# Splitting the keys of a head pair in full-height operations, and filling the doubled tiles by half-token transfers

## The chip, the cores and the metric

The kernel runs on one core of one Trainium2 chip. The metric is the device time of one execution in microseconds (us). Before the change the median of three runs is 1488.08 us (1487.84 to 1490.82).

## What is computed

A two-layer encoder trunk over 1024 tokens of width 1024, in fp32. Layer 0 has global attention (8 query heads, 2 key heads), windowed attention (8 and 2) and attention into 256 memory tokens; layer 1 has 16 heads of neighbourhood attention on a 16 x 64 grid, and memory attention. The keys that the change concerns are those of the windowed attention (one pair of heads) and of the neighbourhood attention (eight pairs). The reference, cut to these:

```python
def reference(x, mem, ...):
    ...
        if l % 2 == 0:
            qa, ka, va, qb, kb, vb, qm, gate = split_cols(h @ w_in_even[e], SPLIT_EVEN)
            ...
            yb = window_gqa(qb.reshape(B, S, 8, 64), kb.reshape(B, S, 2, 64), vb.reshape(B, S, 2, 64), sink_b[e], rel_bias)
            ym = memory_attn(...)
            y = jnp.concatenate([ya, yb, ym], axis=-1) * jax.nn.silu(gate)
            x = x + y @ w_out_even[e]
        else:
            qc, kc, vc, qm, gate = split_cols(h @ w_in_odd[o], SPLIT_ODD)
            yc = neighborhood_attn(qc.reshape(B, S, 16, 64), kc.reshape(B, S, 16, 64), vc.reshape(B, S, 16, 64), rpb_c[o])
            ym = memory_attn(...)
            y = jnp.concatenate([yc, ym], axis=-1) * jax.nn.silu(gate)
            x = x + y @ w_out_odd[o]
    return rmsnorm(x, final_norm_gain)
```

## The kernel before, in words

Every fp32 operand of a matmul is kept as a high and a low part (fp32r); a product is the sum of high x high, high x low and low x high. TensorE (PE) does all products and transposes, ScalarE (ACT) copies the high part out of PSUM, VectorE (DVE) subtracts it from the source to get the low part, GpSimd (POOL) scales softmax rows and splits weights, SyncE (SP) issues nearly all transfers from one queue in program order.

A head has 64 channels, and a pair of heads fills 128 partitions. To do high and low of the query in one matmul, the query tile of a head holds its high part in one half of the partitions and its low part in the other; the key tile must then hold the same 64 key rows in both halves. So `k_pair` (line 345) makes four tiles of 128 x 1024 for a pair: high and low of head 0, high and low of head 1, each with its 64 rows twice. It projects 512 tokens at a time into a PSUM tile `pj`; for each 512 its `sink` makes, per head, a 64-row ACT copy (the high part, recorded at the helper's line L125) and a 64-row DVE subtraction (L361). After the second 512 four transfers of 64 x 1024 inside SBUF (L366 the high part, L367 the low, both named `k<-k`) copy each head's rows to the other half of its tiles.

`k_pair` is called once in layer 0 (`even`, with `natural=True`: the tokens are put in grid order, from an SBUF tile `vt`) and eight times in layer 1 (`keys(j)` in `odd`). There the projections of later pairs are broken in steps and run as filling work between the attention steps of the pair before. `near` runs the attention: scores of step n (`s<-k,q`, 16 steps a pair, 8 per head, head 0 first), softmax on DVE, ACT and POOL, transposes `tr<-ident,pn`, the split of the transposed rows into `ph` and `pl` (L125 and L542), products `pv`, and at the end of each half head `close`, whose DVE addition (L1158) writes the pair's output tile `yb`. There are two `yb` tiles, so a pair waits in `close` until the output of the pair two before it has left: `gated_steps` (line 470) gates it, sends the sums (L492), loads another pair's rows (L493), and sends two more differences (L500, and L503 which is the last to read `yb`).

The order of each engine's rows is fixed when the program is built, by a scheduler that goes by priorities and its own timeline; the queue of SP is in that order too, and a transfer that has to wait holds up all that stand behind it.

Of the kernel before, what the change touches and what calls it, by code (L numbers as in the profile page):

```python
# [9 lines left out]
F32 = mybir.dt.float32  # L10
# [3 lines left out]
OP = mybir.AluOpType  # L14
# [4 lines left out]
T = 1024  # L19
# [28 lines left out]
            c=(("P", "P"), ("P", "P"), ("P", "P"), ("yb", "yb"))),  # L48
       dict(y=(("P", "P", "q", "q", "v"), ("k", "k", "k", "k", "q", "q"), ("H",) * 6, ("H",) * 6, ("P", "P", "q", "q", "v"),
               ("k", "k", "k", "k", "q", "q"), ("H",) * 6),  # L50
            c=(("H", "H"), ("H", "H"), ("mk", "sg"), ("yb", "yb"))))
# [13 lines left out]
class Trunk:  # L65
# [279 lines left out]
    def k_pair(self, w, nt, natural=False):  # L345

        nc = self.nc
        ks = []

        def sink(p, c, n):  # L350
            if not ks:
                ks.extend([self.st("k", [128, T], F32R) for _ in range(2)] for _ in range(2))
            kh, kl = zip(*ks)
            p = self.with_rstd(p, c, n)[:, :n]
            if natural:
                p = p.rearrange("p (b r c) -> p b r c", r=16, c=8)
            for i in range(2):
                s = slice(64 * i, 64 * i + 64)
                h, l = (self.columns(t[i], c, n, natural) for t in (kh, kl))
                self.copy(h[s], p[s])  # L360
                nc.vector.tensor_tensor(l[s], p[s], h[s], op=OP.subtract)  # L361
            if c + n < T:
                return
            for i in range(2):
                s, o = slice(64 * i, 64 * i + 64), slice(64 - 64 * i, 128 - 64 * i)
                nc.sync.dma_start(kh[i][o, :].bitcast(F32), kh[i][s, :].bitcast(F32))  # L366
                nc.sync.dma_start(kl[i][o, :].bitcast(F32), kl[i][s, :].bitcast(F32))  # L367
        self.tokens(w, nt, sink)
        return ks

# [1851 lines left out]
```

## Time and profile before

| | |
|---|---|
| median of three runs | 1488.08 us |
| profiled execution: span from first to last instruction | 1486.8 us |
| around the span, against the median | 1.3 us |
| PE busy | 1467.6 us (99%) |
| DVE, ACT, POOL busy | 1030.7, 837.2, 644.2 us |
| transfers of the SP queue | 270.20 MB |
| neighbourhood attention and its key projections | about 1107 to 1357 us |

The profiled execution has no time of its own beside its span; 1.3 us is the median of the runs less the span, and is added to a span where a time is given. An instruction is named by engine, source line, output and inputs (`DVE L361 k<-pj,k` is the subtraction in `k_pair`). SPq is the queue of SP. In a list of waits or a timeline, `<-` and a name say what ended an engine's idle time. "To landing" is the time from the issue of a transfer to its arrival.

### The profile page before, as it was taken

The page shows a single profiled execution, that of the slowest core. Times are in us where ns is not written, and L with a number is a line of the kernel's source. Part 1 is how long each engine was busy: PE and PEld are TensorE (multiplying, and loading weights), DVE is VectorE, ACT ScalarE, POOL GpSimd, SP SyncE. Part 2 cuts the span into 40 slices and gives each one's busy share as a digit, 9 for nine tenths or more (in the row PEclk, how much of TensorE's full clock was granted, in tenths as well). Part 3 has the DMA queues.
Part 4 walks back from the last instruction along what each step waited for, and adds up shares of the span by engine and source line. Part 5 has one row for each costly group of instructions (what it writes and reads, how often), then busy time and mean ns, then how long its engine had stood idle before and what let it go on. Part 6 is the DMA issues. An engine that isn't in the chain of part 4 may idle for free.

```text
span 1486.8 us, 25511 instructions
## 1 busy us (share of the span) xinstructions
PE 1467.6 (99%) x8433; PEld 1274.7 (86%) x8433; DVE 1030.7 (69%) x2124; ACT 837.2 (56%) x1877; POOL 644.2 (43%) x767
## 2 busy tenths in 40 slices
PE   9999999999999999999999999999999999999998
PEld 8898898988888788888879987888998898888886
DVE  6687777677776577776687776664446787778674
ACT  7743665556655456654544444444446777777454
POOL 1223668556765746543450000001425556665454
PEclk9999999999999999999999999999999999999999
DMA  8966334434443424388553343567665568789834
GB/s 287 306 160 181 118 125 160 123 120 133 126 137 112 155 78 144 100 276 303 187 176 127 128 135 137 157 169 241 233 242 170 188 198 269 246 283 323 314 105 144
DMA packets 173860, 271.92 MB, mean 183 GB/s; under 512 B 15648, under 2 KB 96800, under 8 KB 172704
## 3 DMA queue, kind: packets, MB, share of 16 engines
q1 hardware_dynamic: 173296, 270.20, 56.4%
q8 instruction: 67, 1.10, 0.3%
q14 instruction: 65, 0.53, 0.1%
q10 hardware_dynamic: 432, 0.09, 0.0%
HBM read 174.28 MB, written 83.89 MB: 174 GB/s over the span
## 4 chain that ended last, share of the span: by engine, by line
PE 86%; DMA 6%; DVE 3%; ACT 2%; issue 1%; SPq 1%; POOL 1%; POOLq 0%; ACTq 0%; DVEq 0%
PE pj L242 16%; PE pj L62 11%; PE x L1617 6%; PE tr L133 6%; PE pv L1066 4%; PE y L1617 4%; PE pv L62 3%; PE s L62 3%; PE pj L1332 3%; PE tr L62 3%; PE sa L1332 2%; PE pv L1617 2%; PE sa L1033 2%; PE s L1332 2%; PE sa L1034 2%; PE pj L851 2%
## 5 line engine op out<-in xcount | busy, mean ns | idle before, releaser
L542 DVE TENSOR_TENSOR pl<-tr,ph 128x512 fp32r<-128x512 f32 (+2 forms) x352 | 203.9, 594 | 45.5 <-ACT ph L125 43.6
L125 ACT ACTIVATE ph<-tr 128x512 fp32r<-128x512 f32 (+2 forms) x352 | 176.2, 522 | 103.7 <-PE tr L133 79.7
L242 PE MATMUL pj<-H,wh 128*128 128x512 f32 x704 | 233.2, 411 | 0.6 <-DVE vt L313 0.2
L158 POOL TENSOR_SCALAR wh<-wraw 128x512 fp32r<-128x512 f32 x48 | 32.2, 673 | 275.2 <-PE x L1617 236.0
L125 ACT ACTIVATE wh<-wraw 128x384 fp32r<-128x384 f32 (+1 forms) x163 | 88.7, 553 | 99.6 <-PE pj L1332 12.2
L242 PE MATMUL pj<-H,wl 128*128 128x512 f32 x352 | 139.2, 395 | 0.0
L242 PEld LDWEIGHTS pj<-H,wh 128*128 128x128 f32 x704 | 120.6, 189 | 19.3 <-issue 0.6
L62 PE MATMUL pj<-H,wh 128*128 128x512 f32 x384 | 121.0, 396 | 0.0
L1119 POOL TENSOR_SCALAR pn<-pn,st 128x384 f32<-128x384 f32 (+1 forms) x128 | 72.7, 569 | 102.1 <-DVE st L1118 62.0
L133 PE MATMUL tr<-ident,P 128*128 128x128 f32 x752 | 115.4, 273 | 0.3 <-POOL P L719 0.2
L1279 POOL TENSOR_TENSOR wl<-wraw,wh 128x384 fp32r<-128x384 f32 x56 | 62.9, 1125 | 91.5 <-ACT wh L125 89.2
L1117 ACT ACTIVATE pn<-pn,st 128x384 f32<-128x384 f32 (+1 forms) x128 | 75.1, 587 | 41.8 <-DVE st L1114 40.5
L133 PEld LDWEIGHTS tr<-ident,P 128*128 128x128 f32 x752 | 88.9, 140 | 8.2 <-POOL P L719 1.2
L1039 ACT ACTIVATE P<-sa,st 128x1024 f32<-128x1024 f32 x64 | 71.4, 1117 | 35.3 <-PE tr L133 19.1
L1041 POOL TENSOR_SCALAR P<-P,st 128x1024 f32<-128x1024 f32 x64 | 74.6, 1169 | 27.9 <-DVE st L1040 27.3
L1038 DVE TENSOR_REDUCE st<-sa 128x1 f32<-128x1024 f32 x64 | 77.5, 1218 | 8.3 <-PE sa L1034 7.6
L62 PE MATMUL s<-k,q 128*128 128x384 f32 (+1 forms) x352 | 81.2, 327 | 0.0
L242 PEld LDWEIGHTS pj<-H,wl 128*128 128x128 f32 x352 | 66.2, 188 | 15.1
L62 PE MATMUL pj<-H,wl 128*128 128x512 f32 x192 | 75.6, 394 | 0.0
L160 POOL TENSOR_TENSOR wl<-wraw,wh 128x512 fp32r<-128x512 f32 x52 | 69.6, 1341 | 10.3 <-ACT wh L125 7.8
L851 PE MATMUL pj<-ah,H 128*128 128x256 f32 x384 | 70.8, 282 | 1.0 <-ACT ah L125 0.6
L62 PEld LDWEIGHTS pj<-H,wh 128*128 128x128 f32 x384 | 66.6, 188 | 5.4
(568 smaller groups left out, 4186.7 us busy)
## 6 DMA issues: line engine op xcount, KB each, us to landing
wraw<-w_o SPq DMA_DIRECT2D x52, 256.0 KB, 3.7
y<-yb SPq DMA_DIRECT2D x24, 512.0 KB, 3.4
wraw<-s SPq DMA_DIRECT2D x64, 192.0 KB, 3.9
wraw<-w_e SPq DMA_DIRECT2D x44, 256.0 KB, 3.3
k<-k SPq DMA_DIRECT2D x42, 256.0 KB, 5.9
s<-bias SPq DMA_DIRECT2D x56, 192.0 KB, 2.0
wq<-w_o SPq DMA_DIRECT2D x40, 256.0 KB, 3.3
y<-sg SPq DMA_DIRECT2D x18, 512.0 KB, 3.5
```

Source lines behind the costliest of these rows:

```text
L62: return lambda *a, **k: self.tc.keep_in_program_order(getattr(self.engine, name)(*a, **k))
L125: return self.nc.scalar.activation(out, in_, AF.Copy, scale=scale)
L133: self.turned = self.fence = self.pe.transpose(o, i, self.ident)
L242: self.pe.matmul(a[:, :n], s[:, kt % UNIT, :], m, start=(kt == 0 and i == 0), stop=(kt == KT - 1 and i == 2))
L542: self.low = nc.vector.tensor_tensor(pl[:, :n], tr[:, :n], ph[:, :n], op=OP.subtract)
L851: self.last = nc.tensor.matmul(a[:, b * 256:(b + 1) * 256], x[kt][:, t], w, start=(kt + b + i == 0), stop=(kt == KT - 1 and i == 2), skip_ ...
L1038: nc.vector.tensor_reduce(st[:, 0:1], s, axis=AX.X, op=OP.max, negate=True)
L1041: self.normal = nc.gpsimd.tensor_scalar(pt, pt, st[:, 2:3], 0.5, op0=OP.mult, op1=OP.mult)
L1117: nc.scalar.activation(o, o, AF.Exp, bias=st[:, 0:1], scale=-1.0, accum_out=st[:, 2:3])
L1119: self.normal = normal = nc.gpsimd.tensor_scalar(o, o, st[:, 3:4], 0.5, op0=OP.mult, op1=OP.mult)
L1332: last = nc.tensor.matmul(bank, s[:, k, :], y[3 * u + k][m][:, cols], start=start and u + k + e == 0, stop=u == 1 and k + e == 4, skip_gro ...
L1617: self.last = nc.tensor.matmul(bank, ws[s][:, k, :], b[k][m], start=start and k + i == 0, stop=k == UNIT - 1 and i == 2, skip_group_check= ...
```

## The change

`sink` now splits all 128 partitions at once: one ACT copy and one DVE subtraction for each 512 tokens (`split`, the helper at line 127), into the two tiles that will be head 1's. A new function `spread` then fills the other halves: `a` is a tile of head 0, `b` the tile of head 1 that holds both heads' rows. Head 0's rows go from `b` to the lower and to the upper half of `a`, and then head 1's rows go from the upper half of `b` to its lower half, over the rows just copied. This is done for the high part and then for the low part. In layer 1 `spread` is called after each 512 tokens (transfers of 64 x 512), in layer 0 once for all (64 x 1024). So a pair has 12 transfers of 128 KB in place of 4 of 256 KB in layer 1, and 6 of 256 KB in place of 4 in layer 0; the third of each three waits until the first two have landed, since it overwrites what they read.

```diff
         ks = []
+        one, two = slice(0, 64), slice(64, 128)
+
+        def spread(c):
+            for a, b in zip(*ks):
+                for t, o, f, i in ((a, one, b, one), (a, two, b, one), (b, one, b, two)):
+                    nc.sync.dma_start(t[o, c].bitcast(F32), f[i, c].bitcast(F32))
 
         def sink(p, c, n):
             if not ks:
                 ks.extend([self.st("k", [128, T], F32R) for _ in range(2)] for _ in range(2))
-            kh, kl = zip(*ks)
             p = self.with_rstd(p, c, n)[:, :n]
             if natural:
                 p = p.rearrange("p (b r c) -> p b r c", r=16, c=8)
-            for i in range(2):
-                s = slice(64 * i, 64 * i + 64)
-                h, l = (self.columns(t[i], c, n, natural) for t in (kh, kl))
-                self.copy(h[s], p[s])
-                nc.vector.tensor_tensor(l[s], p[s], h[s], op=OP.subtract)
-            if c + n < T:
-                return
-            for i in range(2):
-                s, o = slice(64 * i, 64 * i + 64), slice(64 - 64 * i, 128 - 64 * i)
-                nc.sync.dma_start(kh[i][o, :].bitcast(F32), kh[i][s, :].bitcast(F32))
-                nc.sync.dma_start(kl[i][o, :].bitcast(F32), kl[i][s, :].bitcast(F32))
+            self.split(*(self.columns(t, c, n, natural) for t in ks[1]), p)
+            if not natural:
+                spread(slice(c, c + n))
+            elif c + n == T:
+                spread(slice(0, T))
         self.tokens(w, nt, sink)
         return ks
```

The order of PE's rows is the same before and after. ACT and DVE each lose 18 rows, and a few rows beside them change places with a neighbour. The queue of SP gets 66 transfers more (33 listed rows, since two alike that follow each other stand in one row, marked x2) and is rearranged around them. Behind the changed function the line numbers are one lower after the change. Two places matter below.

The first is SP's queue at the start of `near`, where the first pair's keys are made. Before, `k_12667` and `k_12668` are the high and low tile of head 0, `k_12669` and `k_12670` those of head 1; `y_2` is an output row in DRAM, `qc` a stored query.

```order
L1019 DMA q_12894<-qc_9291 128x1024
L521 DMA y_2_85<-sg_12363 128x2x512
L520 DMA y_2_85<-yb_12362 128x2x512
L366 DMA k_12667<-k_12667 64x1024
L367 DMA k_12668<-k_12668 64x1024
L366 DMA k_12669<-k_12669 64x1024
L1989 DMA sg_12973<-g_9274 128x1024
L367 DMA k_12670<-k_12670 64x1024
L138 DMA wraw_13324<-w_o 128x512
```

The same place after; `k_12665` and `k_12666` are now the high and low tile of head 0 (`a`), `k_12667` and `k_12668` those of head 1 (`b`).

```order
L354 DMA k_12665<-k_12667 64x512 x2
L354 DMA k_12666<-k_12668 64x512 x2
L519 DMA y_2_85<-yb_12360 128x2x512
L520 DMA y_2_85<-sg_12361 128x2x512
L1018 DMA q_12900<-qc_9289 128x1024
L354 DMA k_12667<-k_12667 64x512
L354 DMA k_12665<-k_12667 64x512
L354 DMA k_12668<-k_12668 64x512
L354 DMA k_12665<-k_12667 64x512
L354 DMA k_12666<-k_12668 64x512 x2
L1988 DMA sg_12979<-g_9272 128x1024
```

The first half's transfers now stand ahead of the three 512 KB transfers, and two that wait for landings (`k_12667<-k_12667`, `k_12668<-k_12668`) stand ahead of or between those that complete head 0.

The second is SP's queue where the last pair's keys are made. `y_8` is the output whose store frees the `yb` tile for the seventh pair's `close`; the loads from `y_0` to `y_2` are the output projection's first operands. Before:

```order
L492 DMA y_8_91<-yb_14699 128x1024
L493 DMA sg_14737<-y_2_85 128x1024
L1231 DMA k_16037<-y_0_83 128x1024
L1019 DMA v_15687<-v_106 128x2048
L1231 DMA k_16038<-y_1_84 128x1024
L1081 DMA bm_15650<-offsets 128x640
L1231 DMA q_16039<-y_2_85 128x1024
L1291 DMA wraw_16269<-w_oo 128x384
L500 DMA y_8_91<-sg_14737 128x1024
L503 DMA y_8_91<-yb_14699 128x512
L366 DMA k_15597<-k_15597 64x1024
L367 DMA k_15598<-k_15598 64x1024
```

And after:

```order
L354 DMA k_15623<-k_15625 64x512 x2
L354 DMA k_15624<-k_15626 64x512 x2
L1080 DMA bm_15680<-offsets 128x640
L1018 DMA v_15717<-v_106 128x2048
L1230 DMA k_16067<-y_0_83 128x1024
L354 DMA k_15625<-k_15625 64x512
L354 DMA k_15626<-k_15626 64x512
L1230 DMA k_16068<-y_1_84 128x1024
L1230 DMA q_16069<-y_2_85 128x1024
L1290 DMA wraw_16299<-w_oo 128x384
L499 DMA y_8_91<-sg_14759 128x1024
L502 DMA y_8_91<-yb_14721 128x512
```

The two rows `y_8<-yb` and `sg<-y_2` that open the first list stand just ahead of this one too. Six transfers of the first half (0.75 MB) now stand ahead of the last store of `y_8`; the four that complete head 0 (`k_15623` and `k_15624`) follow right behind it, where two of 256 KB stood.

## The prediction

> **What bounds the kernel now.** I read the page first, then PE's waits in the stretch where eight of the nine key pairs are made (1100 to 1330 us), then the busy times there.
>
> ```profile
> PE 1467.6 (99%) x8433; PEld 1274.7 (86%) x8433; DVE 1030.7 (69%) x2124; ACT 837.2 (56%) x1877; POOL 644.2 (43%) x767
> ```
> ```profile
> PE tr L62 <- DVE pl L542: 0.9, 2, 0.6
> ```
> ```profile
> 1107.00:1125.00 18.00, 18.00 (x104) 15.64 (x103) 9.45 (x21) 10.12 (x27) 4.00 (x6) 1.00 0.87 298
> 1297.00:1327.40 30.40, 29.82 (x179) 26.34 (x178) 24.77 (x77) 22.74 (x62) 19.02 (x25) 1.00 0.74 250
> ```
>
> The first row says that PE is the bound. The wait list of the stretch holds this one line (who waits and for whom, us in total, times, longest): in 230 us PE waited 0.9 us, in two places. The window rows give stretch, length and busy time of PE, weight loads, DVE, ACT, POOL (instructions in brackets), then granted clock, DMA share and GB/s. PE is busy 18.00 of 18.00 us where the first pair is made and misses 0.58 us in the stretch that ends at the last pair, at a granted clock of 1.00. So PE's work, which the change leaves alone row for row, sets the time; only new PE waits or those 0.9 us can move it there.
>
> **The change, part by part.** First the operations that go. These are groups of DVE and ACT by shape, with count, busy us and mean ns.
>
> ```profile
> L361 DVE TENSOR_TENSOR k<-pj,k 64x512 fp32r<-64x512 f32 x32 | 22.0, 686 | 5.9 <-ACT k L125 5.4
> L313 DVE TENSOR_TENSOR vt<-pj,rows 128x512 f32<-128x512 f32 x10 | 6.8, 685 | 8.8 <-PE pj L242 8.8
> L125 ACT ACTIVATE k<-pj 64x512 fp32r<-64x512 f32 x32 | 18.9, 591 | 8.8 <-PE pj L62 7.1 <-DVE k L361 1.1
> L125 ACT ACTIVATE ph<-tr 128x512 fp32r<-128x512 f32 x184 | 109.1, 596 | 74.4 <-PE tr L133 71.8 <-issue 0.2
> L361 DVE TENSOR_TENSOR k<-vt,k 64x512 fp32r<-64x512 f32 x4 | 3.5, 867 | 1.4 <-ACT k L125 1.3
> L125 ACT ACTIVATE k<-vt 64x512 fp32r<-64x512 f32 x4 | 2.5, 629 | 0.1
> ```
>
> Full height costs no more than half height (685 against 686 ns on DVE, 596 against 591 on ACT). So half of each group goes: DVE 16 x 0.686 + 2 x 0.867 = 12.7 us, ACT 16 x 0.591 + 2 x 0.629 = 10.7 us. All of it lies beside a busy PE, so it gives PE at most its waits of 0.9 us; I count it as nothing. If that cover were gone it would be worth those 12.7 us, but no row shows PE waiting for a `k` split.
>
> In layer 0 the two added transfers and their waits come at about 490 us. Head 0's tile, which is read first, needs no waiting transfer, and what is queued behind them are weights loaded ahead of their split and stores. I cost it at zero; if a load there were late by a landing without cover, PE would lose up to the 6.4 us quoted below.
>
> Next the transfers of layer 1: 1.5 MB a pair for 1.0 MB. The queue that carries them is full at the first and the last pair and has gaps between (DMA share 1.00 and 0.99 there):
>
> ```profile
> 1107.00:1118.40 11.40, 11.40 (x68) 9.93 (x67) 7.04 (x14) 7.15 (x21) 3.69 (x5) 1.00 1.00 372
> 1307.80:1312.00 4.20, 4.20 (x29) 3.71 (x28) 4.00 (x11) 3.17 (x9) 1.17 (x2) 1.00 0.79 268
> 1312.00:1326.00 14.00, 14.00 (x83) 12.29 (x81) 10.98 (x36) 10.37 (x28) 9.18 (x12) 1.00 0.99 346
> ```
>
> First pair. SP's timeline (start, us) and PE's first scores of `near`, then the same transfers' size and time to landing:
>
> ```profile
> 1109.15 0.37 SPq L521 DMA_DIRECT2D y<-sg  x1
> 1109.87 0.37 SPq L520 DMA_DIRECT2D y<-yb  x1
> 1115.11 0.51 SPq L366 DMA_DIRECT2D k<-k  x1
> 1115.83 0.50 SPq L367 DMA_DIRECT2D k<-k  x1
> 1122.88 0.40 PE L62 MATMUL s<-k,q 128*128 128x256 f32 x2
> ```
> ```profile
> y<-sg SPq DMA_DIRECT2D x1, 512.0 KB, 7.9
> y<-yb SPq DMA_DIRECT2D x1, 512.0 KB, 8.5
> ```
> ```profile
> k<-k SPq DMA_DIRECT2D x1, 256.0 KB, 4.3
> ```
> ```profile
> k<-k SPq DMA_DIRECT2D x1, 256.0 KB, 4.7
> ```
>
> Issue plus landing: the stores arrive at 1117.05 and 1118.4, head 0's high part at 1119.4, its low part at 1120.5, and PE reads them at 1122.88. The slack is 2.4 us. The two copies arrive 1.1 us apart, so a `k<-k` takes about 1.05 us of a full queue per 256 KB, and I take 0.53 us for a piece of 128 KB. After the change ten pieces (six of the first half, four of the second) must pass, beside the same three transfers of 512 KB, before head 0 is complete: 10 x 0.53 - 2 x 1.05 = +3.2 us, so 1123.7, and PE waits 0.8 us. Bounds for a piece: the stores above pass 512 KB in 1.4 us, 0.34 us for 128 KB, and then the copies arrive at 1121.8 with no wait; if a piece cost as much as a whole transfer (1.05 us) they arrive at 1128.9 and PE waits 6.0 us. I take half the measured copy, since it is the same transfer with rows half as long, and keep 0 and 6.0 as ends.
>
> Here a rule of the Trainium skill speaks the other way. "DMA: Bandwidth & Descriptors", section "Where 436 GB/s comes from", states that transfers between SBUF and SBUF are bound by the fabric at about 435 GB/s; by it a piece is an estimated 0.30 us, the sum +1.8 us or less and the first pair in time. The row says 256 KB in 1.05 us, 250 GB/s, so the trace does not agree, and I keep the row.
>
> Last pair. The `yb` tile for the seventh pair comes free with the last store of an earlier output:
>
> ```profile
> 1319.31 0.32 SPq L503 DMA_DIRECT2D y<-yb  x1
> 1320.07 0.47 SPq L366 DMA_DIRECT2D k<-k  x1
> 1321.08 0.47 SPq L367 DMA_DIRECT2D k<-k  x1
> 1324.98 0.68 DVE L1158 TENSOR_TENSOR yb<-pv,bt 64x512 f32<-64x512 f32 x1 [1.26 <-DMA y<-yb]
> 1326.68 0.98 PE L62 MATMUL tr<-ident,pn 128*128 128x128 f32 x6 [0.58 <-DVE pl L542]
> 1327.42 0.36 PE L62 MATMUL s<-k,q 128*128 128x256 f32 x1
> ```
> ```profile
> y<-yb SPq DMA_DIRECT2D x1, 256.0 KB, 5.5
> ```
> ```profile
> k<-k SPq DMA_DIRECT2D x1, 256.0 KB, 5.9
> ```
>
> The store lands at 1324.8, DVE has stood idle 1.26 us for it, the splits behind are late and PE loses 0.58 us; head 0's low part lands at 1327.0, 0.4 us before its use. After, six pieces stand ahead of that store: 6 x 0.53 = 3.2 us, less the room that the queue still has at 1307.8 to 1312 (0.21 x 4.2 = 0.9), so +2.3 us. DVE and with it PE have nothing left to give: PE waits 2.3 us more. Head 0's copies, the same 0.5 MB behind the store, come 2.3 us later as well and their use too, so no second wait. Ends: with 0.34 us a piece 6 x 0.34 - 0.9 = +1.1, with 1.05 us +5.4.
>
> One border gains. The same store for the pair before stood behind two `k<-k` that were long to issue; it now goes ahead of those that wait:
>
> ```profile
> 1285.83 2.05 SPq L366 DMA_DIRECT2D k<-k  x1
> 1287.93 1.36 SPq L367 DMA_DIRECT2D k<-k  x1
> 1289.38 0.54 SPq L503 DMA_DIRECT2D y<-yb  x1
> 1294.66 0.68 DVE L1158 TENSOR_TENSOR yb<-pv,bt 64x512 f32<-64x512 f32 x1 [1.75 <-DMA y<-yb]
> 1296.76 0.52 PE L62 MATMUL tr<-ident,pn 128*128 128x128 f32 x3 [0.33 <-DVE pl L542]
> ```
>
> Those two hold the queue for 2.05 + 1.36 us; up to 3.4 us earlier, so DVE's 1.75 and PE's 0.33 us go: -0.3. Had it no such effect, 0.
>
> Last, the waits of SP: before each third piece it must stand until two have landed, 34 times (for high and low part in 16 halves of layer 1 and once in layer 0). That it can stand for a landing, this row shows: 53.6 us in 32 waits.
>
> ```profile
> SPq L1255 <- DMA s<-bias: 53.6, 32, 3.7
> k<-k SPq DMA_DIRECT2D x32, 256.0 KB, 6.4
> ```
>
> By the second (median landing) a wait here is up to some 6 us, twice for each half. What stands behind are loads of queries, values, bias and weights for coming heads and pairs, and head 1's own tile, read 8 of 16 steps after head 0's, half of a pair's time (1297.0 to 1327.4 above is the seventh pair, 30.4 us). I cost it at nothing beside the two places above.
>
> Sum: +0.8 + 2.3 - 0.3 = +2.8 us on the span of 1486.8, so 1489.6, and with 1.3 us around it 1490.9.
>
> **The rivals.** (1) The transfers stay hidden. For it: PE has 2.4 us of slack at the first pair, and with 0.34 us a piece there is no wait there; the store may also be served earlier than its turn. Against: the full queue. Then only 0 to +1.1 at the last pair less 0.3: about 1488.2. The skill's fabric rate would lead to this case too. (2) SP's waits decide. A third piece is held, and behind it a transfer that is soon needed. The nearest is the fifth pair:
>
> ```profile
> 1226.34 0.47 SPq L367 DMA_DIRECT2D k<-k  x1
> 1237.61 0.36 PE L62 MATMUL s<-k,q 128*128 128x256 f32 x1
> ```
> ```profile
> k<-k SPq DMA_DIRECT2D x1, 256.0 KB, 8.4
> ```
>
> Head 0 lands there at 1234.7, 2.9 us early. It decides from 2.9 us of added delay; one wait of 6 us on top would give +3 us there, so about 1494. Against: head 0's pieces are issued before any of the same half that waits. (3) Faster, the other side: the shorter chain ACT, DVE, ACT, DVE (2.6 us a half by the means above, now 1.3) lets the scores' softmax run earlier. It decides only where PE waits for DVE or ACT, which is 0.9 us in the stretch; all of it gone and no delay gives 1487.2. To be faster by over 0.2% it would need 3 us, which no row offers.
>
> **How the numbers follow.** 0.2% (3.0 us, about what this kernel's timing can tell from no change) is 1485.1 to 1491.1. Late keys and store, as summed: 0.52, spread 1489.0 to 1494.5 by the ends of the piece, with a little under half of it over 1491.1. Hidden: 0.28. SP's waits: 0.15, all slower. Faster: 0.05, 0.03 of it beyond 0.2% (for a cause that no row shows). Slower is then 0.24 + 0.15, faster 0.03, the same 0.58. The range runs from the hidden case with every wait gone to that of SP's waits, 1487.0 to 1495.0; both upper ends of the piece together (+11 us) I give 0.04, inside the first case.
>
> **What would show it.** 16 + 2 fewer operations on each of DVE and ACT, the full-height ones at about 0.69 and 0.59 us; PE's first `s<-k,q` of `near` waiting about 0.8 us for `k<-k`; at the last border DVE waiting about 3.5 us for `y<-yb` and PE some 2.9; at the border before, no such wait. Wrong would be: PE's waits in the stretch unchanged (the pieces are cheaper or hidden), or waits for `k<-k` at other pairs (SP's blocking counts).

## The result and the profile after

The changed kernel takes 1493.89 us (median of 12 runs, 1489.57 to 1497.29) against 1487.39 us for the kernel before (12 runs, 1486.18 to 1490.82): a ratio of 1.004, interval 1.0029 to 1.005. It is slower by 0.4%. The prediction said 1490.9 us and held the same time within 0.2% the most likely (0.58), slower less so (0.39). The time lies inside its range of 1487.0 to 1495.0, but 3.0 us above the forecast and on the less likely side. Its profiled execution took 1493.11 us, its span is 1491.3.

Two rows of the page, then PE's waits from 1100 to 1330 us, then the groups of the key splits:

```profile
PE 1469.6 (99%) x8433; PEld 1277.7 (86%) x8433; DVE 1021.7 (69%) x2106; ACT 828.5 (56%) x1859; POOL 641.3 (43%) x767
...
k<-k SPq DMA_DIRECT2D x96, 128.0 KB, 3.8
```
```profile
PE pv L62 <- DVE st L1117: 2.8, 1, 2.8
PE tr L62 <- POOL pn L1118: 0.7, 2, 0.5
```
```profile
L129 DVE TENSOR_TENSOR k<-pj,k 128x512 fp32r<-128x512 f32 x16 | 11.0, 686 | 3.9 <-ACT k L125 3.9
L125 ACT ACTIVATE k<-pj 128x512 fp32r<-128x512 f32 x16 | 9.5, 592 | 6.8 <-PE pj L62 6.7
```

DVE and ACT have 18 operations fewer each, as counted; their busy time falls by 9.0 and 8.7 us. Where PE had lost 0.9 us to DVE in this stretch it now loses 2.8 us at one place and 0.7, in two waits, at another. (The list names DVE's row L1117, which directly follows the addition that PE waits for.) The first place, in the timelines of SP, DVE and PE at the last border, and then PE's busy time, the granted clock and the queue in three windows (columns as in the prediction's window rows):

```profile
1315.30 1.64 SPq L354 DMA_DIRECT2D k<-k  x2
...
1318.66 1.34 SPq L499 DMA_DIRECT2D y<-sg  x1
1321.37 0.32 SPq L502 DMA_DIRECT2D y<-yb  x1
1323.02 2.66 SPq L354 DMA_DIRECT2D k<-k  x4
```
```profile
y<-yb SPq DMA_DIRECT2D x1, 256.0 KB, 7.4
```
```profile
1328.89 0.68 DVE L1157 TENSOR_TENSOR yb<-pv,bt 64x512 f32<-64x512 f32 x1 [3.11 <-issue]
```
```profile
1326.47 0.48 PE L62 MATMUL s<-k,q 128*128 128x256 f32 x2
1329.72 0.35 PE L62 MATMUL pv<-ph,v 128*128 128x256 f32 x1 [2.77 <-DVE st L1117]
```
```profile
1326.70:1329.70 3.00, 0.25 (x3) 0.05 (x2) 0.81 (x3) 0.31 (x2) 0.00 (x0) 1.00 1.03 350
1329.70:1331.50 1.80, 1.78 (x9) 1.67 (x10) 1.80 (x6) 1.54 (x4) 0.48 (x1) 0.93 0.96 362
1331.50:1334.30 2.80, 2.80 (x8) 2.11 (x8) 0.72 (x5) 0.71 (x2) 2.08 (x3) 0.50 1.00 320
```

The store that frees the `yb` tile is issued at 1321.37 and lands 7.4 us later, at 1328.8; before it was 1319.31 and 1324.9. DVE's addition starts with the landing (the profile names no releaser, "issue"), and PE stands 2.77 us. Then comes what no term had: from 1331.5 to 1334.3 PE is busy all the time at a granted clock of 0.50, where its 128x512 matmuls start 0.43 us apart in place of 0.23.

Since PE's rows are the same in both kernels, one by one, the start of each row after less its start before gives PE's lateness:

| at (us, before) | lateness of PE | change | place |
|---|---|---|---|
| 1107 | -0.56 | | `near` begins |
| 1124 | -0.56 | 0 | first pair: no wait |
| 1256 | +0.47 | +1.03 | between fifth and sixth pair |
| 1297 | +0.02 | -0.45 | border before the last: its wait is gone |
| 1328 | +1.98 | +1.96 | last border: the stand |
| 1331 | +3.57 | +1.59 | half clock behind it |
| 1481 | +4.56 | +0.99 | later: PE waits 0.6 us for a weight's split at 1396 |

So of 4.5 us of span, 3.6 were lost within 5 us at the last border.

### The profile page after: what moved, and what is told of

Its sections match the earlier page's. It is cut to its first block, busy times and chain, and to the rows that moved or that the text cites. A ratio compares the mean times of both kernels' runs of the same rounds, so it can differ in the third digit from the quotient of the medians.

```text
span 1491.3 us, 25562 instructions
## 1 busy us (share of the span) xinstructions
PE 1469.6 (99%) x8433; PEld 1277.7 (86%) x8433; DVE 1021.7 (69%) x2106; ACT 828.5 (56%) x1859; POOL 641.3 (43%) x767
## 4 chain that ended last, share of the span: by engine, by line
PE 51%; DMA 2%; issue 1%; POOL 1%; DVE 0%; SPq 0%; ACT 0%; POOLq 0%; DVEq 0%
PE pj L62 12%; PE x L1616 6%; PE y L1616 4%; PE pv L62 3%; PE s L62 3%; PE pj L1331 3%; PE tr L62 3%; PE sa L1331 3%; PE pv L1616 2%; PE tr L1331 2%; PE s L1331 2%; PE pv L414 2%; PE y L414 1%; PE sa L1344 1%; PE pv L1331 1%
```

## The experiments

Four kernels ran on the same chip at a time, each batch with its own runs of the kernel before, whose medians were 1490.26 (first four), 1488.59 (next four) and 1488.80 us (last four). Ratios are to these; times in the expectations were set against 1487.4 or 1488.6 and are read as differences.

| run | what | ratio | interval |
|---|---|---|---|
| e1 | change in all pairs but the last | 1.001 | 0.9998 to 1.0022 |
| e2 | change in the last pair only | 1.0031 | 1.0019 to 1.0043 |
| e3 | old split, old bytes, in half-token transfers | 1.0011 | 0.9999 to 1.0023 |
| e4 | new split, whole-token transfers | 1.0055 | 1.0042 to 1.0069 |
| e5 | change, third transfers once at the end | 1.0044 | 1.0029 to 1.0059 |
| e6 | change, third `yb` tile | 1.0052 | 1.0037 to 1.0066 |
| e7 | before, third `yb` tile | 1.0008 | 0.9997 to 1.0019 |
| e8 | change again | 1.004 | 1.0023 to 1.0058 |
| e9 | before, 0.5 MB more sent in the last pair | 1.0035 | 1.002 to 1.0049 |
| e10 | before, 0.5 MB more sent in the third pair | 1.0009 | 0.9993 to 1.0024 |
| e11 | change, last pair's keys made earlier | 1.0004 | 0.9989 to 1.002 |
| e12 | before, last pair's keys made earlier | 0.9999 | 0.9984 to 1.0013 |

### Which pair: e1 and e2

```diff
+            if nt == O_K + 7:      # e1; e2 has !=
+                ... the old body: 64-row splits, four transfers at the end
+                return
             self.split(*(self.columns(t, c, n, natural) for t in ks[1]), p)
```

> The changed kernel, with the last of the eight pairs of layer 1 made in the old way (64-row splits, four transfers of 256 KB at the end). Theory A: what is lost lies at the last border, where the first half's six pieces of the last pair stand ahead of the store that frees the yb tile (4 of the 5 us that the profile shows lost from the start of the neighbourhood attention on). Then DVE's wait there is 1 to 2 us again, PE's 0.5 to 1, and the time is 1488 to 1490: the fifth pair's 1 us may stay. Rival B: the waits of SP and the added transfers cost at many places, a little each; then this kernel loses most of it still, 1491.5 to 1493.5.

> The kernel before, with only the last pair of layer 1 made in the new way (full-height split, twelve transfers of 128 KB). Theory A (the last border): PE stands there 2.5 to 3 us, and runs at half its clock for some 3 us after it as in the changed kernel; 1491 to 1493. Rival B (many places): at most a fifth of the loss, 1488 to 1489.

The last pair alone gives 1.0031 of the 1.004. All the others together give 1.001, some 1.5 us, with an interval from no change to 3.3 us. PE's waits from 1240 us on, e1 and then e2 (line numbers behind the function are 14 higher here):

```profile
PE tr L62 <- POOL pn L1132: 2.4, 1, 2.4
PE tr L62 <- DVE pl L555: 1.4, 2, 1.1
```
```profile
PE pv L62 <- DVE st L1131: 2.4, 1, 2.4
PE pj L62 <- DMA v<-y: 0.7, 2, 0.4
PE pj L1358 <- ACT wh L125: 0.6, 1, 0.6
PE tr L62 <- DVE pl L555: 0.5, 2, 0.4
```

e2 repeats the last border: a stand of 2.4 us, and half clock from 1332.0 to 1335.4 us. In e1 PE stands 1.1 us there and keeps its full clock. Its profiled execution has a 2.4 us wait between the fifth and the sixth pair, with half clock behind it, so 4 us there; as its ratio is 1.001, this is not what it usually costs. Theory A (the last border) stands, B (many places) falls.

### Which part of it: e3 and e4

In layer 1, e3 keeps the old split and sends its four transfers for each half (8 of 128 KB a pair); e4 has the new split and calls `spread` once for all tokens (6 of 256 KB).

```diff
-                nc.sync.dma_start(kh[i][o, :].bitcast(F32), kh[i][s, :].bitcast(F32))   # e3
+                nc.sync.dma_start(kh[i][o, d].bitcast(F32), kh[i][s, d].bitcast(F32))   # d: this half
...
-            if not natural:                                                             # e4
-                spread(slice(c, c + n))
-            elif c + n == T:
+            if c + n == T:
                 spread(slice(0, T))
```

> The old split (64 rows at a time, no tile filled twice, no transfer that waits for another), but its transfers sent for each half of the tokens: 8 of 128 KB a pair in place of 4 of 256 KB, the same bytes. Four pieces of the last pair's first half stand ahead of the store. Theory A1 (what stands ahead of the store, by bytes): 4 x 0.35 = 1.4 us later, 1488.5 to 1489.5. A2 (the wait before each third piece holds SP): there is none, so 1487 to 1488. A3 (the number of transfers: SP issues one only when the eighth before it has landed): four more in the row, two thirds of the changed kernel's loss, 1490 to 1492.

> The changed kernel's split, but the tiles filled once for all 1024 tokens: 6 transfers of 256 KB a pair, all behind the last pair's yb store in SP's order. The same bytes as the changed kernel, half the transfers. Theory A: the store lands as in the kernel before (DVE waits some 1.3 us, PE under 1); but head 0 is complete only after four transfers of 256 KB in place of two, some 2 us later, so PE waits up to 1.7 us for k<-k at the last pair, 1488.5 to 1490. By bytes alone (rival B, 0.5 MB more a pair wherever it is sent): as the changed kernel, 1492 to 1494.

PE's waits from 1240 us on, e3 and then e4:

```profile
PE pv L62 <- DVE yb L1159: 2.0, 1, 2.0
PE pj L62 <- DMA v<-y: 0.6, 2, 0.3
```
```profile
PE s L62 <- DMA k<-k: 3.3, 2, 1.7
PE pj L62 <- DMA v<-y: 2.9, 1, 2.9
...
```

e3, without added bytes, lies at 1.0011, where A1 put it, but its interval reaches from no change to 1.0023, so the time does not separate A1 from A2 and hardly from A3. The trace says more: there is no third piece that SP could stand for, and yet the store is late by 2.5 us (8.07 us from GpSimd's last difference to the landing, for 5.57 before), which is more than A1's 1.4. It was issued at once (1316.63 us, GpSimd done at 1316.61), so the delay lies on its way. PE stands 2.0 us for it, with half clock behind. e4 was missed by all theories. The store is early there (3.90 us), the `yb` wait is gone as A said, and the kernel is with e6 the slowest of all: PE waits 3.3 us for head 0's keys, and then 2.9 us at a place that no theory had named, for `v<-y`, an operand of the output projection. Taking the loss from one place put it at another.

### Taking the waits away: e5 to e8

```diff
-                for t, o, f, i in ((a, one, b, one), (a, two, b, one), (b, one, b, two)):   # e5
+                for o in (one, two):
+                    nc.sync.dma_start(a[o, c].bitcast(F32), b[one, c].bitcast(F32))
+            if c.stop == T:
+                ... b[one, :] <- b[two, :] for both
...
-            ... pn=8, ph=4, pl=4, sg=1, yb=2, ...                                           # e6, e7
+            ... pn=6, ph=4, pl=4, sg=1, yb=3, ...
```

> The changed kernel, but the third transfers (head 1's rows to the lower half, over what the others read) are sent once for all 1024 tokens, behind the second half: SP no longer stands for landings in the middle of a pair. Theory A: at the fifth pair (some 1250 us), where SP stood for two landings with an output's store and a gate load behind it, GpSimd's stand of 5 us and PE's loss of 1 us go; at the last border four pieces in place of six stand ahead of the store, at 0.62 us each (store late by 2.5 in place of 3.7 us), so PE stands 1 to 2 us there: ratio 1.001 to 1.003. Rival B (SP's waits cost nothing, the bytes alone count): same bytes, as the changed kernel, 1.004.

> The changed kernel with a third yb tile (and two score tiles pn fewer, for room), so that no pair waits in close for a store. Theory A: DVE's wait for y<-yb at the last border goes, and with it PE's stand of 2.8 us and the 1.6 us at half clock behind it. Head 0's pieces of the second half land some 1.8 us before their use, so nothing takes its place: ratio 0.999 to 1.0015 (the fifth pair's loss may stay). Rival C (the keys of the last pair are late too, hidden behind the store): PE waits for k<-k in place of it, ratio 1.002 to 1.004.

> The kernel before with the same third yb tile and two pn fewer. Its own waits at the two last borders are 0.9 us in all: 0.999 to 1.000. Less room for scores may cost something, then both this and the changed kernel with a third tile lose it.

> The changed kernel once more, for its times on the chip of these runs and a second profile: ratio 1.003 to 1.005. Theory A: at the last border PE stands 2 to 3 us, then half the clock for some 3 us. At the fifth pair GpSimd's stand for the gate load may cost PE 1 us as in the first profile or 4 as in the run with the last pair in the old way; before 700 us a loss may show or not (it comes in runs of either kind).

The expectations that theory A gave on e5 and e6 failed in the time. In e6 the wait went as said; in e5 the stand at the border shrank to 0.4 us, and the loss at the fifth pair stayed. By its time e5 is where rival B (the bytes alone) put it, while e6 is slower than both A and C had it. PE's waits from 1240 us on, e5 and then e6, and PE at the place:

```profile
PE pj L62 <- DMA v<-y: 3.1, 2, 2.5
PE pj L1347 <- ACT wh L125: 1.5, 1, 1.5
PE tr L62 <- POOL pn L1121: 0.7, 2, 0.6
PE pv L62 <- DVE yb L1160: 0.4, 1, 0.4
...
```
```profile
PE pj L62 <- DMA v<-y: 3.0, 2, 2.7
PE tr L62 <- POOL pn L1118: 1.2, 2, 1.0
```
```profile
1351.69 0.73 PE L62 MATMUL pj<-v,wh 128*128 128x512 f32 x2 [2.52 <-DMA v<-y]
```

With SP's waits in mid-pair gone (e5) the store comes in time, 0.4 us of wait; with a third tile (e6) nobody waits for it. In both PE runs on to the place that reads `v<-y` (it stops at 1349 us in e5, at 1354 in e6), stands there, and pays half clock behind that stand. At the fifth pair e5 still loses 0.7 us in waits, as the changed kernel does, so SP's standing was not the cause there. e7 shows that the third tile itself (with two score tiles fewer) costs at most 0.2%. e8 repeats the change (1.004), with a stand of 4.0 us at the last border.

Theory D follows: what is scarce from 1310 to 1350 us is the queue. Windows of 10 us from 1300 on, the kernel before:

```profile
1300.00:1310.00 10.00, 10.00 (x62) 8.98 (x61) 8.00 (x25) 6.38 (x19) 6.48 (x9) 1.00 0.28 92
1310.00:1320.00 10.00, 10.00 (x64) 9.01 (x63) 8.24 (x29) 8.38 (x24) 7.40 (x10) 1.00 0.93 334
1320.00:1330.00 10.00, 9.41 (x54) 8.02 (x53) 8.47 (x27) 7.10 (x20) 3.99 (x7) 1.00 1.02 337
1330.00:1340.00 10.00, 10.00 (x62) 8.98 (x61) 7.33 (x24) 7.45 (x19) 7.66 (x9) 1.00 1.02 367
1340.00:1350.00 10.00, 10.00 (x63) 8.96 (x62) 7.54 (x26) 7.91 (x21) 3.72 (x8) 1.00 1.03 384
```
```profile
PE pj L62 <- DMA v<-y: 0.2, 1, 0.2
```

The DMA share is 0.93 to 1.03 for 40 us, and at its end PE already waits 0.2 us for `v<-y`: there was no slack at 1350 us before anything was changed. In every run so far that added bytes to the queue in these 40 us PE paid for them: at the store (the change, e2, e8), at `v<-y` (e5, e6), or at the keys and at `v<-y` (e4).

### The queue by itself: e9 to e12

e9 and e10 leave split and tiles as before and only add transfers; e11 and e12 move the last pair's projection ahead of half a gate's, and load that gate's rows later.

```diff
+            if nt == O_K + 7 and c == 0 and not natural:        # e9; e10 has O_K + 2
+                for i in range(2):
+                    for t in (kh, kl):
+                        d = self.dr.tile([64, 512], F32, name=self.name("extra"))
+                        nc.sync.dma_start(d, t[i][64 * i:64 * i + 64, 0:512].bitcast(F32))
...
-                    ... (O_K + 6, keys(6)), half(6, 512), (O_K + 7, keys(7)), ...            # e11, e12
+                    ... (O_K + 6, keys(6)), (O_K + 7, keys(7)), half(6, 512), ...
```

> The kernel before, and in the last pair four transfers more, sent when the first half is split: the four 64x512 blocks just written go to an unused place in DRAM as well (0.5 MB, the bytes that the change adds to a pair; nobody reads them and no transfer waits for them). Theory D, formed after the runs so far: from some 1310 to 1350 us the queue is full, PE meets it at the yb store (1325 us) and at the loads v<-y of the output projection (1350 us) with no slack in the kernel before, so time added to the queue there is paid in full, and a stand of over 1.5 us costs 1.6 us more at half clock. By 0.4 to 0.6 us a transfer that is 1.6 to 2.4 us of stand, with the half clock up to 4: ratio 1.001 to 1.003, and v<-y lands 1.5 to 2.5 us later beside PE's work. Rival: it is the waiting third pieces or the new split that cost, not the load of the queue: 1.000.

> The same four transfers more, but in the third pair (some 1140 to 1170 us), where the queue has gaps. Theory D: no effect, ratio 0.999 to 1.001. Rival (0.5 MB cost wherever they are sent): as with the four in the last pair.

> The changed kernel, with the last pair's key projection made ahead of the second half of the seventh gate's projection in place of behind it (and that gate's load some 18 us later). Its twelve pieces then go some 11 us earlier, when the queue was about a third full (1300 to 1310 us). Theory D: less stands ahead of the yb store and of v<-y, both land 2 to 4 us earlier beside PE's work; ratio 1.000 to 1.002. Rival (the pieces cost the same wherever they go): 1.004.

> The kernel before with the same move of the last pair's keys. Theory D: its waits of 0.9 us at the two last borders shrink to 0 to 0.5, ratio 0.999 to 1.000; it can hardly be told from the kernel before. Rival: the gate or the store is late in the new order, 1.001 to 1.002.

e9, with none of the change in it, is as slow as the change within the intervals; its size is a little over what D gave. (The 1.5 us that D names for the half clock do not hold as a bound: stands of 1.6 to 1.8 us in e1, e5 and e6 kept the full clock.) PE's waits of e9 from 1240 us on, and then the first two windows of e11:

```profile
PE s L62 <- issue: 1.9, 1, 1.9
PE tr L62 <- DVE pl L547: 1.2, 3, 0.5
PE s L62 <- DMA k<-k: 0.9, 1, 0.9
```
```profile
1300.00:1310.00 10.00, 10.00 (x61) 8.95 (x60) 7.46 (x25) 6.54 (x19) 3.20 (x6) 1.00 0.74 224
1310.00:1320.00 10.00, 10.00 (x62) 8.93 (x61) 7.97 (x26) 6.97 (x19) 10.00 (x13) 1.00 0.88 260
```

In e9 PE meets the queue at the last pair's keys: it stands 1.9 us until the moment when head 0's high part lands, 0.9 more for the low part, and has half its clock from 1332 to 1335 us. The same four transfers in the third pair (e10), where the queue of the kernel before is at 0.50 (1140 to 1150 us) and 0.82 (to 1160), give 1.0009, an interval that holds no change; its upper end (1.0024) just meets e9's lower (1.002). In e11 six of the last pair's pieces go out from 1297.9 to 1304.7 us, where the queue had room (0.28 above), and six from 1309.3 to 1313.5; now it is at 0.74 from 1300 to 1310 and at 0.88 after, DVE does not wait for `yb` at the last border, `v<-y` costs PE 0.3 us, and the ratio falls from 1.004 to 1.0004. The move helps the border in a second way, though: GpSimd's last difference, which the store waits for, ends at 1314.0 us in e11 for 1319.5 in the changed kernel. So e11 shows that another order takes the loss away, and not how much of that the place of the pieces does. What is left in its profile is 2.4 us at the fifth pair. e12 shows that the move itself brings the kernel before nothing that can be measured: no version here beats it.

## Why the prediction was right, and where not

**Bound.** That new PE waits would move the time held, but not that only they could: 1.59 us came while PE was busy, at half its clock. And the prediction looked at PE's waits up to 1330 us, where the attention's keys end, and so did not see that the full queue goes on to 1350 and that PE meets it there with 0.2 us of wait already (the step "in 230 us PE waited 0.9 us, in two places" was cut too short).

**Operations that go.** Right: 18 fewer on each of DVE and ACT, at 686 and 592 ns, worth nothing. (The busy time of the two engines fell by 9.0 and 8.7 us and not by the 12.7 and 10.7 of the sum: the groups of the split shrank by 12.4 and 10.7, on DVE the weights' splits took 3.0 us longer, and the rest is not worked out.)

**First pair, +0.8 us.** Wrong; it measured 0. The step that failed is that PE must wait until all ten pieces have passed and head 0 is complete. Their price was near: the last of them lands at 1123.5 us (1118.21 + 5.3, below) for a forecast of 1123.7. But PE starts at 1122.32, before that. The first scores read tokens 0 to 255 only, and with a transfer for each half PE waits for the half that it reads. The fourth step (1126.03 us) is the first that reads beyond token 511, 3.7 us after the first.

```profile
1118.21 0.60 SPq L354 DMA_DIRECT2D k<-k  x1
```
```profile
k<-k SPq DMA_DIRECT2D x1, 128.0 KB, 5.3
```
```profile
1122.32 0.40 PE L62 MATMUL s<-k,q 128*128 128x256 f32 x2
...
1126.03 0.51 PE L62 MATMUL s<-k,q 128*128 128x384 f32 x2
```

**Last pair, +2.3 us.** The mechanism was right, store, `yb`, DVE, PE, and so was the stand: 1.96 us more than before. Two sizes behind it were off, and 2.1 us of DVE's work that nobody had counted came in; that they nearly cancelled is luck. A transfer of 128 KB ahead of the store delayed it by 0.62 us and not 0.53 ((9.28 - 5.57) / 6 in the changed kernel, (8.07 - 5.57) / 4 in e3, (8.00 - 5.57) / 4 in e9, all from GpSimd's last difference to the landing; 0.52 in e2 and 0.74 in e8). In e5 four pieces delayed it by only 0.5 us in all, so how much of it is SP's standing for third pieces is not settled. And the 0.9 us of room that was subtracted was not to be had: the store came 3.7 us later, 1.8 of them before it was issued (GpSimd was done at 1319.53, the issue is at 1321.37; the last section says why). Of all this PE lost only 1.96, because the order of DVE's rows had changed too. Before, DVE comes to the addition from a key split; after, from a softmax row that ends at 1325.78 in place of 1323.72 us, so that 2.1 us of other work were done ahead of the stand. Before and after, the last row of DVE ahead of the addition:

```profile
1323.03 0.69 DVE L361 TENSOR_TENSOR k<-pj,k 64x512 fp32r<-64x512 f32 x1
```
```profile
1325.62 0.16 DVE L1117 RECIPROCAL st<-st 128x1 f32<-128x1 f32 x1
```

Missing altogether is the term behind the stand, 1.59 us at half clock. The claim that DVE and PE "have nothing left to give" was too strong, and "no second wait" held only for the keys.

A row for this term was there. In the kernel before, at the end, PE stands (1.6 us between 1478.5 and 1480.4) and the clock falls:

```profile
1478.50:1480.40 1.90, 0.31 (x4) 0.26 (x4) 1.80 (x7) 0.52 (x3) 1.47 (x2) 1.00 0.27 95
1480.40:1481.20 0.80, 0.56 (x4) 0.32 (x4) 0.54 (x2) 0.20 (x1) 0.48 (x1) 0.79 1.09 384
1481.20:1484.00 2.80, 0.00 (x0) 0.00 (x0) 1.46 (x3) 0.18 (x1) 1.26 (x1) 0.50 1.09 383
```

The prediction priced waits at their length. The Trainium skill, "TensorE: Matmul & The Clock Gate", section "Part 1: The HAM clock gate", states the rule: PE's clock drops to 4/8 after an idle window of some 3.4 us. The traces agree on the half (0.50) and not on the length: stands of 1.2 to 2.9 us were enough here, the shorter ones not always (last section).

**Border before, -0.3 us.** Right: -0.45.

**SP's waits, 0.** Right in effect, with a wrong doubt. A third piece does hold SP, and at the fifth pair the gate load behind it went out 3.4 us later (1244.85 for 1241.48) and GpSimd stood 5.1 us for it:

```profile
1242.50 1.39 SPq L354 DMA_DIRECT2D k<-k  x2
1244.00 0.51 SPq L491 DMA_DIRECT2D y<-yb  x1
1244.85 0.33 SPq L492 DMA_DIRECT2D sg<-y  x1
```
```profile
1250.46 1.30 POOL L496 TENSOR_TENSOR sg<-yb,sg 128x512 f32<-128x512 f32 x1 [5.10 <-DVE st L1117]
```

(The row names DVE; the load landed at 1250.3 us, just ahead of GpSimd's start.) That is rival 2 at another place than it was put, and cost PE 1.03 us. But e5 sends that load at 1242.32 and it lands at 1249.19, still 3.0 us later than before: there too it was the queue's load. The term of zero stood for 1.0 us in this execution; over many, e1's 1.001 (none to 3.3 us) bounds what all the pairs but the last cost.

**The sum.** +2.8 us on the span was forecast, +4.5 came in the profiled execution: -0.8 for the first pair, -0.5 at the two borders, +1.6 of half clock, +1.0 at the fifth pair, +1.0 behind the last border; the rest, -0.6, lies ahead of `near`. So the place of the greatest loss was foreseen, and the time fell inside the range in part by luck: the upper end stood for SP's waits, which did not decide. The median is 6.5 us over that of the kernel before; of the difference to 4.5 only this can be said, that single executions of either kernel differ by several us, and that stands of 1 to 2 us ahead of 700 us, with half clock behind some, show in some profiles of both kinds of kernel and not in others. Why they come and go is open, and so is why the fifth pair costs 1 us in one execution and 4 in another.

**The rule that was weighed.** By the fabric rate of the Trainium skill ("DMA: Bandwidth & Descriptors", "Where 436 GB/s comes from") a piece would be an estimated 0.30 us. The last four of head 0 do land 0.32 us apart on average (1329.09 to 1330.06), near that rate; but as something ahead of another transfer a piece added 0.62 us. For the sum made here the second number counts, and the row was nearer to it.

## What to carry to other kernels

Follow a full queue to where it empties, and list every place on the way where an engine meets it, with its slack: bytes added in that stretch were paid for in every run, and taking away the wait that showed them only moved it to the next place (e4, e5, e6). A transfer that spares cheap, hidden engine work costs nothing that shows here only where the queue has gaps (e10), or where the order is changed with it (e11). Price a stand of PE of 2 us or more at its length plus some 1.6 us for the clock behind it, and count a shorter one as a risk of the same.

## What was not expected of the hardware

- **The clock falls after short stands.** In the fourteen traces, between 30 us and the last stand of each kernel, PE stood nine times for 2.0 us or more (up to 4.0). Behind eight of these stands the granted clock was 0.50, each time for 3.41 us, beginning 0.1 to 1.5 us after work had started again; that is some 1.6 us lost. It is not a matter of length alone: the ninth, 2.2 us (e11, at 1253 us), had no such effect, and of 24 stands of 1.0 to 2.0 us only 8 were followed by it (two of them, in e4, by the same fall), the shortest of 1.2 us (e2, at 225 us).
- **At most eight transfers of SP's queue are under way, and the program itself sees to it.** In the traces of both kernels no transfer is issued before the eighth ahead of it has landed (951 and 1017 transfers, no exception), and 69 and 63 go out within 0.12 us after it. The program has eight semaphores for the landings of this queue, and in these traces SP always waits for the last landing on one before it uses it again; whether the queue would take more no run here shows. The store at 1321.37 us is such a case: GpSimd was done at 1319.53, but the 1 MB load `v<-v`, eight ahead, landed only at 1321.31. So a small transfer takes one of eight places just as a large one does. SP's waits from 1320 to 1322 us have this line for the store:

```profile
SPq L502 <- DMA v<-v: 1.3, 1, 1.3
```

- **A transfer's price in a full queue goes by more than its bytes.** Pieces of 64 rows by 2 KB delayed the store behind them by 0.5 to 0.75 us for 128 KB (the change, e2, e3, e8, e9; 0.1 in e5), about twice the 0.32 us at which they land one after another.
